# A branch hint, one block ahead, for the branch that skips each expert's overflow block

## The chip, the cores and the metric

The kernel runs on one core of one Trainium2 chip. The metric is the device time of one execution in microseconds (us); the kernel before took 1608.27 us in the median of three executions (1607.67 to 1610.89).

## What is computed

Two transformer blocks over 256 tokens of 1024 features, batch 1, in float32. The first block has two layers: gated linear attention and a mixture of experts, then a linear recurrence (LRU) and a second mixture of experts. The second block is a merge of three mixers and a convolutional feed-forward. What the change touches is the mixture of experts: a router picks experts for each token, and each of 16 experts computes, for its own tokens,

```python
# per expert e, for the tokens routed to it
y = (silu(x @ w_gate[e]) * (x @ w_up[e])) @ w_down[e]
out[token] += weight * y
```

How many tokens an expert gets is known only when the kernel runs.

## The kernel before, in words

The function `moe` (line 826) runs twice, once per layer. Each expert has 64 fixed slots for tokens: `gather` (L864) brings the tokens of four experts into slots by a product with a one-hot matrix, `gate_up` (L875) multiplies the slots with the gate and up weights, `transp` (L884) turns the result, `down` (L914) multiplies with the down weights, ScalarE (L922) and VectorE (L925) scale the result into two parts `y`, and `scatter` (L931) adds them onto the accumulator in PSUM. An expert with more than 64 tokens needs 32 slots more: the overflow block, that is `block_x` (L959 to L977), `block_up` (L984 to L991) and `block_down` (L998 to L1005). An expert with more than 96 tokens needs a loop over further blocks, `blocks` (L1014 to L1030).

Whether the overflow block runs is decided on the chip. `nblk` holds the number of extra blocks of each expert, every engine loads it into a register (L844), and a `tc.If(vals[e] > 0)` makes all five engines branch. For three experts of each layer, e = 0, 1 and 15 (`split`), the block is cut in two tests: gathering and the up product at L1049, the down product at L1068. For the other thirteen there is one test, at L1068. So an engine meets 19 tests per layer and 38 in all. Where the test is false the engine jumps over the code of the block to a short arm that only counts up its semaphore (the EVENT_SEMAPHORE rows of L1068 and L1049), and goes on behind it.

The code is straight-line: nothing but these tests and the loop inside `blocks` jumps. A scheduler orders the instructions of each engine between two tests; it moves none across a test. So, on TensorE (PE), after the test of one expert come typically the scatter of that expert, the transposes of the next expert's hidden values, most of the gate-up product of the one after, the down product, and the next test.

The weights (2 MB tiles, three per expert) are loaded by SyncE (SP) through one DMA queue in the order of use, into nine tiles during a mixture; `self.ws.free(3)` at an expert's end lets the loads of a later expert start.

Of the kernel before, what the change touches and what calls it, by code (L numbers as in the profile page):

```python
# [145 lines left out]
class Stream:  # L146
    """the weights in the order of their use, loaded ahead into as many tiles as there are"""
# [5 lines left out]
    def add(self, pool, n, until=None):  # L153
        """n tiles of the pool, for the weights before those named `until`"""
        if until:
            self.until[pool] = until
        self.open += [pool] * n
        self.fill()
# [38 lines left out]
class Banks:  # L197
    """the PSUM in two pools, for tiles of two names"""
# [8 lines left out]
class Act:  # L207
    """activations [features, tokens] as two float32r parts whose sum they are"""
# [6 lines left out]
class Half:  # L215
    """features in two tiles of 4"""
# [9 lines left out]
class Acts(Act):  # L226
    """an Act in four tiles"""
# [6 lines left out]
class Net:  # L234
# [39 lines left out]
    def weights(self, n, until=None):  # L274
        """n more tiles for the weights before the mark `until`"""
        self.wB.close()
        if n:
            p = self.wB.enter_context(self.tc.tile_pool(name="wB", bufs=n, side="right"))
            self.ws.add(p, n, self.marks.get(until))
# [112 lines left out]
    def lru_rates(self, pool):  # L392
        """-8 * softplus(-lambda) / 2, and half the gates' biases: sigmoid(z) is (1 + tanh(z / 2)) / 2"""
        nc = self.nc
        cl = self.cl = self.const.tile([P, 8], F32, name="cl")
        cm = pool.tile([P, 8], F32, name="cm")
        lam = self.p("lru_lambda")
        nc.scalar.activation(cl, lam, AF.Abs)
        nc.scalar.activation(cl, cl, AF.Exp, scale=-1.0)
        nc.scalar.activation(cl, cl, AF.Ln, bias=1.0)  # L400
        nc.vector.tensor_scalar(cm, lam, -1.0, 0.0, op0=OP.mult, op1=OP.max)
        nc.vector.tensor_tensor(cl, cl, cm, op=OP.add)
        nc.vector.tensor_scalar(cl, cl, -4.0, None, op0=OP.mult)
        for n in ("lru_b_r", "lru_b_i"):
            nc.vector.tensor_scalar(self.p(n), self.p(n), 0.5, None, op0=OP.mult)

# [1 line left out]
    def conditions(self, pool):  # L408
        """the conditions c, c_2 and c_ctx_2 after their silu, as columns of the array"""
        nc = self.nc  # L410
        s = self.cond = pool.tile([P, KT, 32], F32, name="cond")
        nc.vector.memset(s, 0.0)
        for i, n in enumerate(("c", "c_2", "c_ctx_2")):
            nc.scalar.activation(s[:, :, i], self.p(n), AF.Silu)

    def mod_tile(self, name, j, ps, sb):
        """512 of the modulation vectors, for each of the conditions; the columns of the array take a part of the sum each"""
# [21 lines left out]
    def rsqrt(self, out, x, sb, factor=None):  # L439
        """out = factor * x ** -0.5, x positive: a guess from the exponent and three steps of Newton"""  # L440
# [15 lines left out]
    def rstd(self, out, sums, n, sb, factor=None):  # L456
        """out = factor * (sums / n + eps) ** -0.5, for each token"""
# [4 lines left out]
    def sumsq_by_4(self, x, lhs, n, ps, sb):  # L462
        """[tokens, 2, n]: the squares of x, weighted with the first n columns of the 32 of lhs(k), summed over the
        features; the columns of the array take a part of the sum each"""
# [23 lines left out]
    def sumsq_steps(self, x, ps, sb):  # L488
        """the same into the PSUM, a feature tile at a time: the squares of all but the last tile are added up before"""
# [20 lines left out]
    def rows(self, col, ps):  # L510
        """[any partition, tokens] (PSUM) from [tokens, 2]"""
# [10 lines left out]
    def norm_mod(self, h, x, g, shift, scale, ps, sb, g0=None, between=None, st=None, rw=None):  # L522
        """h = modulated rmsnorm of x; in two parts if h is an Act; with g0, x is first replaced by its rmsnorm;
        between is called between the halves of the features; st: the sums of the squares, rw: the tokens' factors, if
        they are there"""
# [42 lines left out]
    def ctx_norm(self, hc, mc, ps, sb):  # L568
        """hc = modulated rmsnorm of the context, which comes with the weights"""
# [47 lines left out]
    def proj_T(self, out, pc, act, k0=0):  # L617
        """out [128 features, tokens] from a piece [features in, 128 features]"""
# [4 lines left out]
    def lin_T_by_k(self, w, act, ps):  # L623
        """lin_T with one act, all the products together as the features of the act come"""
# [11 lines left out]
    def lin_T(self, w, acts, ps, n=None, pool=0):  # L636
        """for each 128 columns of the weights: a product with each of acts; the low parts of the first `pool` pieces
        made by GpSimd"""
# [12 lines left out]
    def lin_tok(self, w, act, ps, outs=None, k0=0, k1=8):  # L651
        """[tokens, 512] for both tiles of tokens"""
# [24 lines left out]
    def open_route(self):  # L677
        """what a mixer shares with the routing after it"""
# [5 lines left out]
    def gla(self):  # L684
        nc, tc = self.nc, self.tc
        with ExitStack() as st:
# [23 lines left out]
            # the bias as a 17th row  # L710
# [115 lines left out]
    def moe(self, l, m, late, aside={}):  # L826
        nc, tc = self.nc, self.tc
        shift, gate = m[:, 24:32], m[:, 40:48]
        with ExitStack() as st:
# [59 lines left out]
            def slots_of(e, pt):  # L889
                """[slot, token]: 1 where the slot is the token's"""  # L890
# [7 lines left out]
            def slot_w(g):  # L898
                """the weights of the slots, for the experts of a group"""
# [8 lines left out]
            def down(heT, wd, wsl):  # L908
# [9 lines left out]
                # both parts of the results below each other, for one pass  # L918
# [25 lines left out]
            def tokens_of(oo, rk):  # L944
                """[token, slot]: 1 where the token is the slot's; rk: ranks less those of the slots before"""
# [4 lines left out]
            def block_x(e, oo):  # L950
                """32 more slots of an expert whose weights are there.
                A quarter of the features, at last of the results, on each 32 of the array's columns"""
# [61 lines left out]
            def blocks(e):  # L1014
                """the slots of an expert from the 97th on"""
# [16 lines left out]
            # all the products onto zeros, whether the banks count as written or not  # L1032
# [6 lines left out]
            for e in range(NE):  # L1039
# [5 lines left out]
                split, end = e in (0, 1, NE - 1), e == NE - 1  # L1045
                tokens_of(oo, rank64[:, e, :])
                he, last = gate_up(lambda k: XG[g][:, k, j, :], W[e])
                if split:
                    with tc.If(vals[e] > 0):  # L1049
                        blocks(e)  # L1050
                        block_x(e, oo)
                        block_up(e, "pgu")
                    self.ws.free(3 if more else 2)
                pt = ps.tile([P, 512], F32, name="ps")
                heT = transp(he, pt)
# [12 lines left out]
                with tc.If(vals[e] > 0):  # L1068
# [15 lines left out]
    def route_ahead(self, l, m):  # L1084
        """what the routing needs of a feature tile of x, to be called with each as soon as it is there"""
# [32 lines left out]
    def route(self, hh, hl, whl, rank, nblk, late):  # L1118
        """the normed tokens [tokens, features] in two parts, without the norm's gain and the modulation; which experts'
        slots they go to (rank), with which weights"""  # L1120
# [21 lines left out]
        def behind(v, n, name):  # L1142
            """how many of the four, of each of n fours, come before each: the larger ones and the earlier equal ones"""
# [28 lines left out]
        # the blocks of 32 slots after the first 64  # L1172
# [21 lines left out]
    def lru(self, m):  # L1194
        nc, tc = self.nc, self.tc
        with ExitStack() as st:
# [34 lines left out]
            # the gates as 2 * sigmoid - 1  # L1231
# [69 lines left out]
    def to_tok(self, dst, src, n, ps):  # L1301
        """dst [tokens, 2, n * 128] from src [features, n, tokens]"""
# [7 lines left out]
    def to_feat(self, dst, src, ps):  # L1310
        """dst [features, 4, tokens] from src [tokens, 2, 512]"""
# [69 lines left out]
    def merge(self, nm, mrg, h, y, ps, mx, first, slots, m=None):  # L1381
        """mrg += 2 * sigmoid(h @ w_gate) * (y @ w_branch); at last m, its half in two parts"""
# [33 lines left out]
    def y_act(self):  # L1416
        """4 tiles of features, in turn in the two halves of a tile"""
# [6 lines left out]
    def scalar_gates(self, nm, act, pc, ea, ps, mx):  # L1424
# [10 lines left out]
        # softplus: of the forget gates' negative, of the steps  # L1435
# [8 lines left out]
        # token rows: forward heads at columns 0..3, backward ones at 32..35  # L1444
# [13 lines left out]
        # cum: up to and with the token; aft: what follows it; tot: the tile's sum; per direction, in a tile of 128  # L1458
# [11 lines left out]
        # the rows of the forget and input gates, and the running maximum over the sequence  # L1470
# [34 lines left out]
    def conv_silu(self, dst, px, cw, ft, cb, mx):  # L1505
        """silu of the convolution; its weights and biases are halved"""
# [7 lines left out]
    def ctx_states(self, hc, gates, ps, mx, norm):  # L1514
        """what the context leaves: the states of both scans in both directions, keys and values"""
# [85 lines left out]
    def decays(self, pr, E, far, near, ncol, colx, prev):  # L1601
        """E[:, 0] over all t from the tile `far` of s, E[:, 1] over the tile `near` of t from the same of s, E[:, 2]
        from before the sequence; pr holds the part of t, in rows"""
# [14 lines left out]
    def masked(self, sm, pq, st, scale):  # L1618
        """scaled scores of the tile st of s: [:, direction, st, t]"""
# [116 lines left out]
    def tok_out(self, y, src, ps):  # L1736
        """y, in features, from src [tokens, 2, 512]"""
# [9 lines left out]
    def ssd(self, hT, L, C, y, ps, mx):  # L1747
# [72 lines left out]
        # gated with silu(z): here twice that, and half in the norm  # L1820
# [46 lines left out]
    def qk_tok(self, dst, pq, nm, rot, mx, scale=None):  # L1867
        """normed (and turned) queries or keys [tokens, 2, 512]; with scale the norm's factor times it, not applied"""
# [114 lines left out]
    # the features in between whose products with w_down follow those of w_up  # L1983
    DOWNS = {1: ((0, 4),), 3: ((4, 4),), 5: ((8, 4),), 7: ((12, 4),), 10: ((16, 4), (20, 2))}

    def ffn(self, h, m2):
        nc, tc = self.nc, self.tc
        with ExitStack() as st:
# [11 lines left out]
            for i in range(11):  # L2000
                w = self.ws.take("up")
                out = lambda: ps.tile([P, 512], F32, name="pd").rearrange("p (a t) -> p a t", a=2)
                if i == 0:
                    # as the features of h come
# [29 lines left out]
                for k0, nk in self.DOWNS.get(i, ()):  # L2034
                    w = self.ws.take("down")
                    # the last ones by features out, to be done with some of them earlier
# [104 lines left out]
```

## Time and profile before

| | |
|---|---|
| median of 3 executions | 1608.27 us (1607.67 to 1610.89) |
| profiled execution: span, first to last instruction | 1602.8 us |
| its own time, span and what lies around it | taken as the median, 1608.3 us: 5.5 us lie around the span |
| first mixture of experts | 219 to 523 us of the span |
| LRU mixer | 523 to 686 us |
| second mixture of experts | 686 to 971 us |
| second block | 971 to 1602 us |
| DMA of instructions, TensorE's queue | 134 packets, 2.20 MB |

How to read it: the profile has each engine's busy time, what ended each wait, and the clock that TensorE was granted as a share of its full rate. PEq, DVEq, ACTq and SPq are the sequencers of the engines, which fetch instructions, branch and count semaphores ahead of what the engine itself computes; PEld is TensorE's loading of weights into the array. A wait "<- issue" is one for which the profile shows no releaser: the instruction was not yet there. Matmuls of float32 appear as two records each.

### The profile page before, as it was taken

How to read it: one execution, taken by the hardware profiler on the slowest of the kernel's cores; microseconds unless marked ns; L12 is line 12 of the kernel's file. 1: busy time of each engine (PE TensorE's matmuls, PEld its weight loads, DVE VectorE, ACT ScalarE, POOL GpSimd, SP SyncE). 2: the span in 40 equal slices, each digit the busy share in tenths (PEclk: the TensorE clock that was granted, in tenths of full speed). 3: DMA queues.
4: the chain of work that ended last, by engine and by line, in shares of the span. 5: the costliest groups of instructions: out<-in, count | busy, mean ns of one | idle time of the engine just before them, and what ended most of it. 6: DMA issues, size and time to landing. Idle time of an engine off the chain costs nothing. (4 is left out here: it accounts for less than half of the span.)

```text
span 1602.8 us, 23900 instructions
## 1 busy us (share of the span) xinstructions
PE 1453.8 (91%) x9234; PEld 1001.7 (62%) x9234; DVE 806.0 (50%) x1926; ACT 659.6 (41%) x1347; POOL 85.6 (5%) x84
## 2 busy tenths in 40 slices
PE   6999979977878889889887988999999999999999
PEld 3565734333333568634332436888888889889998
DVE  3444432111211776522223125887876787777676
ACT  3634432111211575512121215666664565555553
POOL 0000110000000042200000000000000101400000
PEclk9999989999999999999998999999999999999999
DMA  9998687969999687786979846544643734896400
GB/s 364 387 371 311 222 332 253 350 233 349 354 341 382 218 294 284 279 326 229 392 287 358 319 160 239 187 145 171 205 163 106 262 106 142 301 348 201 142 1 27
DMA packets 193155, 406.44 MB, mean 254 GB/s; under 512 B 4513, under 2 KB 30753, under 8 KB 192690
## 3 DMA queue, kind: packets, MB, share of 16 engines
q1 hardware_dynamic: 192192, 402.75, 69.8%
q8 instruction: 134, 2.20, 0.6%
q10 hardware_dynamic: 754, 0.88, 0.2%
q14 instruction: 75, 0.61, 0.1%
HBM read 402.57 MB, written 1.05 MB: 252 GB/s over the span
## 5 line engine op out<-in xcount | busy, mean ns | idle before, releaser
L604 DVE TENSOR_TENSOR piece<-wt,piece 128x512 fp32r<-128x512 f32 (+1 forms) x364 | 278.0, 769 | 149.3 <-ACT piece L603 147.7
L603 ACT ACTIVATE piece<-wt 128x512 fp32r<-128x512 f32 (+1 forms) x368 | 248.5, 680 | 209.4 <-PE pd L615 158.6
L875 PE MATMUL pgu<-wt,xg 128*64 128x512 f32 x1024 | 266.0, 642 | 25.9 <-PEq L1068 19.8
L875 PEld LDWEIGHTS pgu<-wt,xg 128*64 128x64 f32 x1024 | 77.6, 146 | 162.3 <-issue 152.8
L614 PE MATMUL pd<-hT,piece 128*128 128x256 f32 x624 | 177.7, 285 | 0.0
L615 PE MATMUL pd<-hT,piece 128*128 128x256 f32 x624 | 177.6, 286 | 0.0
L613 PE MATMUL pd<-hT,piece 128*128 128x256 f32 x624 | 177.4, 285 | 0.0
L914 PE MATMUL py<-wt,heT 128*64 128x512 f32 x512 | 130.8, 624 | 5.0 <-ACT heT L886 3.3
L894 DVE TENSOR_SCALAR sa<-ps,par_cst 128x256 fp32r<-128x256 f32 x32 | 15.5, 484 | 231.9 <-issue 170.7
L615 PEld LDWEIGHTS pd<-hT,piece 128*128 128x128 f32 x624 | 118.4, 190 | 3.6 <-issue 1.8
L922 ACT ACTIVATE y<-py,wsl 64x512 fp32r<-64x512 f32 x64 | 43.8, 684 | 185.7 <-PE py L914 168.7
L614 PEld LDWEIGHTS pd<-hT,piece 128*128 128x128 f32 x624 | 118.7, 190 | 2.1 <-issue 2.0
L613 PEld LDWEIGHTS pd<-hT,piece 128*128 128x128 f32 x624 | 118.7, 190 | 1.5 <-issue 1.2
L425 PE MATMUL pd<-wt,cond 128*32 128x512 f32 x576 | 88.4, 630 | 0.9 <-DMA wt<-ada_w 0.9
L914 PEld LDWEIGHTS py<-wt,heT 128*64 128x64 f32 x512 | 39.4, 143 | 74.1 <-issue 68.0
L878 ACT ACTIVATE he<-pgu 128x256 f32<-128x256 f32 x32 | 12.3, 385 | 166.0 <-PE pgu L875 156.7
L931 PE MATMUL acc<-sa,y 128*128 128x256 f32 x256 | 43.5, 309 | 40.2 <-PEq L1068 21.8
L931 PEld LDWEIGHTS acc<-sa,y 128*128 128x128 f32 x256 | 35.2, 201 | 66.5 <-issue 44.9
L613 PE MATMUL pd<-s,piece 128*128 128x256 f32 x224 | 66.2, 297 | 2.3 <-ACT s L1242 2.3
L614 PE MATMUL pd<-piece,hT 128*128 128x512 f32 x160 | 65.8, 412 | 0.1
L615 PE MATMUL pd<-s,piece 128*128 128x256 f32 x224 | 65.0, 294 | 0.7 <-POOL piece L601 0.6
L614 PE MATMUL pd<-s,piece 128*128 128x256 f32 x224 | 64.7, 291 | 0.4 <-DVE s L609 0.4
(591 smaller groups left out, 2936.6 us busy)
## 6 DMA issues: line engine op xcount, KB each, us to landing
wt<-moe_w_gate SPq DMA_DIRECT2D x64, 1024.0 KB, 9.3
wt<-moe_w_up SPq DMA_DIRECT2D x64, 1024.0 KB, 11.6
wt<-moe_w_down SPq DMA_DIRECT2D x32, 2048.0 KB, 13.7
wt<-ada_w SPq DMA_DIRECT2D x24, 2048.0 KB, 16.7
wt<-w_in SPq DMA_DIRECT2D x21, 2048.0 KB, 9.2
wt<-w_mod SPq DMA_DIRECT2D x12, 2048.0 KB, 8.3
wt<-w_up SPq DMA_DIRECT2D x22, 1024.0 KB, 10.0
wt<-gla_w_in SPq DMA_DIRECT2D x6, 2048.0 KB, 19.7
```

The costliest lines, as they stand in the source:

```text
L425: nc.tensor.matmul(acc[32 * c:32 * c + 32, :], self.cond[:, k, :], w[:, k, :], start=(k2 == 0), stop=(k2 == 1))
L603: self.cast = nc.scalar.activation(hi, v, AF.Copy).ins
L604: (nc.gpsimd if low_on_pool else nc.vector).tensor_tensor(lo, v, hi.bitcast(F32), op=OP.subtract)
L613: mm(out, l[0], r[0], start=start, stop=False, **k)
L614: mm(out, l[0], r[1], start=False, stop=False, **k)
L615: mm(out, l[1], r[0], start=False, stop=stop, **k)
L875: last = nc.tensor.matmul(pgu[64 * hf:64 * hf + 64], xg(k), w[k // 4][:, :, k % 4, 256 * hf:256 * hf + 256], start=(k == 0), stop=(k == KT ...
L878: nc.scalar.activation(he, pgu[:, 0, :], AF.Silu)
L894: nc.vector.tensor_scalar(sa, pt[:, :T], self.c("slotcol"), None, op0=OP.is_equal)
L914: nc.tensor.matmul(py[64 * c:64 * c + 64, :], heT[:, b, 64 * hf:64 * hf + 64], wd[:, 2 * hf + b, 512 * c:512 * c + 512], start=(n == 0), s ...
L922: nc.scalar.activation(y[0:64, c], py[h], AF.Copy, scale=wsl[h])
L931: nc.tensor.matmul(acc[:, ft, :], y[:, ft // 4, ft % 4 * P:ft % 4 * P + P], sa, start=False, stop=False, skip_group_check=True)
```

## The change

Each test gets a label, and `mark_branch_hint_location` asks for an instruction BRANCH_PREFETCH_HINT on all five engines that names the test's branch and says that it will likely be taken, that is, that the engine will jump over the block. The instruction names no condition and waits for nothing. The rest of the diff takes comments out of the file.

```diff
@@ in moe, the loop over the experts
                 W[e] = [self.ws.take("moe") for _ in range(3)]
                 split, end = e in (0, 1, NE - 1), e == NE - 1
+                tc.mark_branch_hint_location(f"up{l}_{e}" if split else f"ex{l}_{e}", "LikelyTaken", engines=[mybir.EngineType.PE, mybir.EngineType.SP, mybir.EngineType.DVE, mybir.EngineType.Activation, mybir.EngineType.Pool])
                 tokens_of(oo, rank64[:, e, :])
                 he, last = gate_up(lambda k: XG[g][:, k, j, :], W[e])
                 if split:
-                    with tc.If(vals[e] > 0):
+                    with tc.If(vals[e] > 0, label=f"up{l}_{e}"):
                         blocks(e)
                         block_x(e, oo)
                         block_up(e, "pgu")
                     self.ws.free(3 if more else 2)
                 pt = ps.tile([P, 512], F32, name="ps")
+                if split:
+                    tc.mark_branch_hint_location(f"ex{l}_{e}", "LikelyTaken", engines=[mybir.EngineType.PE, mybir.EngineType.SP, mybir.EngineType.DVE, mybir.EngineType.Activation, mybir.EngineType.Pool])
                 heT = transp(he, pt)
...
-                with tc.If(vals[e] > 0):
+                with tc.If(vals[e] > 0, label=f"ex{l}_{e}"):
                     if not split:
                         block_x(e, oo)
                         block_up(e)
```

Where the hints land is shown by the order of TensorE's instructions. First an unsplit expert in the first layer, from the end of the overflow block before it (the first row is the jump that closes that block) to its own test. Before:

```order
L1068 UNCONDITIONAL_BRANCH
L931 MATMUL acc<-sa,y 128x256 x8
L884 MATMUL ps<-par_pk_70,he 128x128 x2
L875 MATMUL pgu<-wt,xg 64x512 x13
L914 MATMUL py<-wt,heT 64x512 x8
L892 MATMUL ps<-par_pk_70,rank 128x128 x2
L875 MATMUL pgu<-wt,xg 64x512 x3
L844 TENSOR_LOAD nblk
```

And now (the lines of the file are three further down):

```order
L1071 UNCONDITIONAL_BRANCH
L2138 BRANCH_PREFETCH_HINT
L931 MATMUL acc<-sa,y 128x256 x8
L884 MATMUL ps<-par_pk_70,he 128x128 x2
L875 MATMUL pgu<-wt,xg 64x512 x13
L914 MATMUL py<-wt,heT 64x512 x8
L892 MATMUL ps<-par_pk_70,rank 128x128 x2
L875 MATMUL pgu<-wt,xg 64x512 x3
L844 TENSOR_LOAD nblk
L1071 COMPARE_AND_BRANCH
```

The hint is the first instruction that the engine meets after the jump over the block before, and one expert's work lies between it and its branch. No matmul has moved.

Second the split expert 0 of the first layer, between its two tests, as it is now:

```order
L1050 UNCONDITIONAL_BRANCH x2
L2138 BRANCH_PREFETCH_HINT x2
L884 MATMUL ps<-par_pk_70,he 128x128 x2
L914 MATMUL py<-wt,heT 64x512 x8
L892 MATMUL ps<-par_pk_70,rank 128x128 x2
L1071 COMPARE_AND_BRANCH
L998 MATMUL pgu<-wt,oht 32x256 x16
```

Two hints stand together here: the first names the up-test of expert 1, which comes after the one below, and the second names the test L1071 a few rows on. The order of the hinted branches is thus the reverse of the order of the hints. VectorE, ScalarE, GpSimd and SyncE have a hint at the same places, and nothing else differs in their order.

## Rows read from the trace of the kernel before

**Rows 1.** Busy time by stage: first mixture, LRU, second mixture.
```profile
core 0: us, PE busy (x) PEld busy (x) DVE busy (x) ACT busy (x) POOL busy (x), PEclk, DMA share, GB/s
219.00:523.00 304.00, 253.19 (x1302) 106.34 (x1298) 61.27 (x140) 49.33 (x96) 0.00 (x0) 0.93 0.87 320
...
686.00:971.00 285.00, 241.69 (x1183) 100.39 (x1183) 66.64 (x160) 53.90 (x108) 5.08 (x7) 0.95 0.80 294
```

**Rows 2.** Waits of PE: line, releaser, us in total, times, longest us.
```profile
PE acc L931 <- PEq L1068: 21.8, 13, 3.2
PE pgu L875 <- PEq L1068: 19.8, 8, 3.4
...
PE acc L931 <- issue: 11.7, 3, 4.6
...
PE ps L581 <- PEq L1068: 3.4, 1, 3.4
...
PE acc L931 <- PEq L1049: 2.5, 1, 2.5
```

**Rows 3.** Branch records of lines 1068 and 1049: ns minimum, median, maximum.
```profile
L1068 PEldq COMPARE_BRANCH  x33: 78/4979/6330, 224.5 to 965.7; - x33
L1068 DVEq COMPARE_BRANCH  x33: 47/56/63, 230.3 to 969.8; - x33
...
L1049 PEldq COMPARE_BRANCH  x7: 82/1926/6361, 218.7 to 959.8; - x7
```

**Rows 4.** Two single branches of L1068, and the DMA between start and end of each.
```profile
L1068 PEldq COMPARE_BRANCH  x1: 3765/3765/3765, 264.6 to 264.6; - x1
...
DMA packets 1, 0.02 MB, mean 4 GB/s; under 512 B 0, under 2 KB 0, under 8 KB 0
...
L1068 PEldq COMPARE_BRANCH  x1: 6049/6049/6049, 298.6 to 298.6; - x1
...
q1 hardware_dynamic: 841, 2.41, 101.5%
```

**Rows 5.** Straight code, 1003 to 1590 us: TensorE's code packets, and instructions run.
```profile
q8 instruction: 34, 0.56, 0.4%
...
1003.00:1590.00 587.00, 580.67 (x4312) 524.88 (x4311) 450.67 (x1060) 343.97 (x736) 30.63 (x23) 0.99 0.50 169
```

**Rows 6.** Overflow blocks that ran: L990 runs once in each, L984 on pgu if split.
```profile
L984 PE MATMUL pgu<-wt,oxg 128*32 128x256 f32 x64 | 3.7, 381 | 1.0 <-DVE oxg L976 1.0
...
L990 PE MATMUL ps<-par_pk,oxt 128*128 128x128 f32 x3 | 1.0, 328 | 2.2 <-DVE oxt L988 2.2
```

**Rows 7.** Timeline behind the branch of 315.2 us, VectorE and PE: start, us, instruction.
```profile
319.07 1.53 DVE L925 SCALAR_TENSOR_TENSOR y<-py,wsl,y 64x512 fp32r<-64x512 f32 x2 [0.19 <-ACT y L922]
320.63 0.42 DVE L879 TENSOR_TENSOR he<-he,pgu 128x256 f32<-128x256 f32 x1
...
317.83 1.93 PE L875 MATMUL pgu<-wt,xg 128*64 128x512 f32 x6
321.50 0.95 PE L931 MATMUL acc<-sa,y 128*128 128x256 f32 x6 [1.73 <-PEq L1068]
325.81 0.80 PE L931 MATMUL acc<-sa,y 128*128 128x256 f32 x2 [3.37 <-issue]
```

**Rows 8.** The same behind the branch of 418.7 us, PE.
```profile
424.95 1.90 PE L875 MATMUL pgu<-wt,xg 128*64 128x512 f32 x6 [3.03 <-PEq L1068]
```

**Rows 9.** Two stretches at half clock behind such waits; columns as in rows 1.
```profile
306.50:309.90 3.40, 3.40 (x10) 0.96 (x8) 0.00 (x0) 0.18 (x1) 0.00 (x0) 0.50 1.05 381
...
323.60:330.30 6.70, 4.49 (x12) 1.83 (x14) 0.00 (x0) 0.38 (x1) 0.00 (x0) 0.50 1.04 392
```

**Rows 10.** Waits that could come next: weights (PEld), VectorE's branch (PEld), SP's own.
```profile
PEld acc L931 <- DVEq L1068: 15.5, 6, 2.7
...
PEld pgu L875 <- DMA wt<-moe_w_gate: 3.3, 1, 3.3
...
SPq L177 <- PEq L1068: 139.4, 12, 19.7
```

## The prediction

> **What bounds the kernel now.** I read the stages first, then the waits of TensorE (PE), then single branches. By stage, PE is busy for 253.19 of the 304 us of the first mixture of experts and for 241.69 of 285 us of the second [rows 1]: these two stretches hold 51 and 43 us in which PE does nothing, and the granted clock there is 0.93 and 0.95 of full. DMA is at a share of 0.87 and 0.80, so neither stretch is bound by the weights all the time.
>
> The waits name the idle time. PE waits for its own sequencer at the test L1068 before the scatter L931 (21.8 us, 13 times), before the gate-up product L875 (19.8 us, 8 times) and once before L581 (3.4 us), once at L1049 (2.5 us); three more times, 11.7 us in all, it waits in the middle of the scatter for "issue", an instruction that is not there yet [rows 2]. Together 59.2 us.
>
> Why the sequencer is late is in the branch records [rows 3]. On PE one of L1068 takes 4979 ns in the median and 6330 at most, on VectorE 56 ns. The shortest on PE take 78 and 82 ns. What fills the long ones is a load of code: in the branch of 264.6 us, 3765 ns long, one packet of 16 KB is all that any DMA queue moves, and the branch of 298.6 us takes 6049 ns while the weights' queue keeps the 16 engines at 101.5% [rows 4]. So a jump over the block costs a fetch from memory, and the fetch queues behind the weights. In straight code PE's 8623 matmuls and weight loads between 1003 and 1590 us needed 34 such packets [rows 5], 254 instructions each, with PE busy for 580.67 of 587 us: what comes next in the file is loaded ahead, and what lies behind a jump is not. The code that is jumped over is some 500 instructions on PE, two packets: 125 matmul records (8 + 2 + 2 + 64 + 1 + 32 + 16, a float32 matmul being two) with as many weight loads, once in the block and once in its loop.
>
> PE itself does not idle for the whole branch, since its sequencer runs ahead of it: of the 6.0 us behind 315.2 us PE saw 1.73 us [rows 7], behind 418.7 us 3.03 us [rows 8].
>
> **The change part by part.** It adds 38 hints per engine, and removes and moves nothing else. If a hint makes the code behind the jump come early, the branch should fall from about 5 us to near the 0.08 us of one that goes straight on [rows 3]; between hint and branch lies about one expert's work, 253.19 / 16 = 16 us [rows 1], against 6.4 us for the slowest branch [rows 3].
>
> *Gain, waits.* The upper end is all of the 59.2 us [rows 2]. Not all can go, since VectorE is late next: behind the branch of 315.2 us PE's idle time begins at 321.50 - 1.73 = 319.77 us, but VectorE finishes y at 319.07 + 1.53 = 320.60 and he at 320.63 + 0.42 = 321.05, and only then comes its own branch of 0.06 us [rows 3, 7]. The scatter needs that y and waits for VectorE's count, which the trace shows as DVEq L1068 six times [rows 10]. About 321.1 - 319.8 = 1.3 us stay in each of the six, 8 us. Where gate-up follows the branch, as at 418.7 us, nothing of the sort is due and the wait goes whole [rows 8]. The 3.37 us at "issue" [rows 7] go too: the sequencer has just landed near the end of a block and waits for the next one, and if it lands 6 us earlier that load is done in time. Taken: 59.2 - 8 = 51.
>
> [...]
>
> *Loss, wrong hints.* Three overflow blocks ran, one of them in a split expert [rows 6]: 4 of the 38 tests go straight on, where the hint says otherwise. Now they cost 0.08 us. If the hinted code has taken the place of the next block, PE waits as in the "issue" waits, 11.7 / 3 = 3.9 us [rows 2]; if not, nothing. Between 0 and 16 us; taken 2 us each, 8.
>
> *Loss, weights.* Up to now PE waits for a weight tile once, 3.3 us, and SP waits for PE to free tiles, 139.4 us in the first mixture [rows 10]. A faster PE frees tiles sooner and so asks more of the DMA: the first mixture keeps it busy for 0.87 x 304 = 264 us, and as much at the highest share seen, 1.05 [rows 1, 9], takes 252 us. With some 40 us less the stretch lasts 264 us, near that floor. Between 0 and 12 us lost; taken 5.
>
> *Loss, paired hints.* Behind the up-test of a split expert two hints stand together, and the one for the later branch comes first. If an engine keeps one hint alone, the later branch has none; the nearest such wait is the 2.5 us at L1049 [rows 2]. Taken 3 us, bounds 0 and 6.
>
> *The hints themselves* cost no more than a branch that goes straight on, 38 x 0.08 = 3 us on each sequencer. Taken as 0: PE's sequencer is ahead by the 3 us or so that separate a branch from the wait it causes, and the other engines wait for PE here. On VectorE, ScalarE, GpSimd and SP a branch takes 0.06 us or less [rows 3] or is off PE's path, so the hints there gain nothing.
>
> [...]
>
> *Sum:* 51 + 18 - 8 - 5 - 3 = 53 us less. The profiled execution has a span of 1602.8 us, and 5.5 us around it if its own time is the median of the three runs, 1608.27: 1608.3 - 53 = 1555. With the bounds of the terms the main case lies between 1529 (51 + 28) and 1591 (51 - 16 - 12 - 6).
>
> **Rivals.** *Half of the hints are lost.* From the hint to the branch PE issues, in an expert without a gather, 60 matmuls (8 + 2 + 32 + 16 + 2) with their weight loads, 120 instructions, and with a gather of eight feature tiles about 200, against 254 per block [rows 5]. So in 47% and 79% of the cases an edge between two blocks lies in between: for the 24 unsplit tests that jump, 18 x 0.47 + 6 x 0.79 = 13. If the load of the next block at the edge throws the hinted one out, only the other eleven gain: 11/24 of 69 us less 5 is 27 us, 1581 us. For it: the trace shows one block loaded ahead, never two. Against it: a hint that can be given an expert earlier would be of little use then.
>
> *Nothing happens.* The hint is not acted on, or names the arm that comes next anyway: 1608 us. For it: no hint ran in the trace of before, so nothing shows that one works. Against it: the branch that it names has a jump only in the arm that skips.
>
> *Slower: the hinted block takes the place of the next one.* On PE, wherever an edge lies between hint and branch, the engine then finds no code at the edge, loads it, drops the hinted block, and waits again at the branch. Each such edge costs the uncovered 3.9 us [rows 2] and its share of clock, 39% of some 3.4 us or 1.3 us [rows 9]: 13 x 5.2 = 68 us more, against 11/24 x 69 = 32 us gained, and 4 wrong hints do not matter beside it: 36 us slower, 1644 us. It decides from about nine such edges on (9 x 5.2 = 47 against 15 x 2.9 = 43). For it: only one block ahead is ever seen loaded, and code loads queue behind the weights [rows 4]. Against it: a hint given early and lost at each edge would defeat itself.
>
> **How the numbers follow.** Main case 0.53; half 0.14; nothing 0.14; slower 0.19. About 0.2%, 3.2 us, is what a measurement of this kernel can tell from no change. Faster is the first two, 0.67; within 0.2% is the third, 0.14; slower 0.19. The likeliest is 1555 us, with 1529 to 1591 of its own. The range reaches up over the half and the nothing cases to 1611 and leaves the slower one out, 0.19: 1530 to 1611.
>
> **What would show it.** Right: the median of PE's branch records falls from 4979 to a few hundred ns; "PEq" and "issue" nearly vanish from PE's waits before L875 and within L931; waits on VectorE's branch or on y of about 1.3 us take their place before L931; the clock rises above 0.97 in both mixtures; the first mixture lasts about 265 us with DMA near a share of 1; PE's code packets stay near the 134 of the table. Half: long branches stay where an edge lies ahead of them. Slower: new "issue" waits amid L875, L914 or L864 and more code packets. The forecast is wrong if branches shrink and the mixtures do not, because the weights or VectorE hold PE; or if they do not shrink.

## The result and the profile after

The changed kernel took 1553.32 us (median of 4 executions, 1551.34 to 1554.58), the kernel before 1608.62 (4 executions): a ratio of 0.9654, 95% interval 0.963 to 0.9677. The forecast was 1555. The profiled execution has a span of 1552.8 us, 50.0 less than before. It took 1554.58 us itself, so only 1.8 us lie around its span, not the 5.5 that the table of before has; if 1.8 holds there too, the execution profiled before took about 1604.6 us (an estimate), less than any of the four. So 55.3 us by the medians and 50.0 by the two profiles are the same change, seen beside a slower and a faster execution of before.

Busy time by stage, first and second mixture; the columns after the length are PE, PEld, DVE, ACT and POOL busy, the granted clock, the DMA share and GB/s:

```profile
219.00:497.50 278.50, 247.30 (x1306) 105.38 (x1306) 61.57 (x141) 49.24 (x96) 0.00 (x0) 0.94 0.92 344
...
663.00:921.00 258.00, 233.75 (x1186) 98.02 (x1185) 67.36 (x163) 53.83 (x108) 5.17 (x7) 0.97 0.87 325
```

Beside [rows 1] the first mixture is 304.0 - 278.5 = 25.5 us shorter and the second 285 - 258 = 27. In both together PE's idle time falls from 50.8 + 43.3 = 94.1 us to 31.2 + 24.3 = 55.5, by 38.6, and its busy time by 5.9 + 7.9 = 13.8: with the same matmuls that is the clock, up from 0.93 and 0.95 to 0.94 and 0.97. The LRU stretch between them is 165.5 us long, 2.5 more than before, and the second block is the same, which leaves the 50.0.

The branch records (ns minimum, median, maximum; the lines of the file moved by up to three):

```profile
L1071 PEldq COMPARE_BRANCH  x33: 74/439/6418, 225.3 to 914.5; - x33
...
L1071 DVEq COMPARE_BRANCH  x33: 47/61/80, 231.1 to 918.6; - x33
...
L1050 PEldq COMPARE_BRANCH  x7: 74/3506/6239, 219.5 to 908.9; - x7
```

The exit test's median on PE went from 4979 ns [rows 3] to 439; but some are still 6.4 us long, and the up-test's median rose. PE's waits (us in total, times, longest):

```profile
PE ps L959 <- issue: 6.7, 1, 6.7
PE pgu L875 <- PEq L1071: 6.4, 8, 3.7
PE acc L931 <- PEq L1050: 5.1, 2, 2.6
...
PE acc L931 <- PEq L1071: 4.4, 15, 0.4
...
PE ps L581 <- DVE oo L947: 3.6, 1, 3.6
...
PE acc L931 <- DVE y L925: 3.0, 2, 2.7
```

Of the 59.2 us of [rows 2], the 41.6 behind L1068 at L931 and L875 are now 10.8, and the 11.7 at issue are 0.4 at L931. Two did not go: the 2.5 at the up-test are 5.1, and the 3.4 at L581 are 3.6 (now put on VectorE's `oo`; a branch of 6.4 us still stands right ahead of it). The wait at L959, 1.3 us before, is 6.7. TensorE's code packets fell from 134 to 122:

```profile
q8 instruction: 122, 2.00, 0.5%
```

How PE now goes through the scatter (ACT's and DVE's y, then PEld and PE; start, us):

```profile
314.76 1.38 ACT L922 ACTIVATE y<-py,wsl 64x512 fp32r<-64x512 f32 x2 [9.27 <-PE py L914]
316.17 1.53 DVE L925 SCALAR_TENSOR_TENSOR y<-py,wsl,y 64x512 fp32r<-64x512 f32 x2 [0.18 <-ACT y L922]
317.14 1.21 PEld L931 LDWEIGHTS acc<-sa,y 128*128 128x128 f32 x8 [1.15 <-DVE y L925]
317.15 1.41 PE L931 MATMUL acc<-sa,y 128*128 128x256 f32 x8 [0.28 <-PEq L1071]
```

It is the expert of [rows 7]. Its 1.73 and 3.37 us are 0.28 and none. The scatter begins at 317.15, before the second half of y is finished at 316.17 + 1.53 = 317.70 and before VectorE's branch: it waits for neither. What TensorE's weight loading waits for, 1.15 us, is the first half of y; PE itself idles for 0.28, which the profile puts on its sequencer.

### The profile page after: what moved, and what is told of

It is laid out like the page before. It is cut to its first block, busy times and chain, and to the rows that moved or that the text cites. A ratio compares the mean times of both kernels' runs of the same rounds, so it can differ in the third digit from the quotient of the medians.

```text
span 1552.8 us, 24090 instructions
## 1 busy us (share of the span) xinstructions
PE 1439.3 (93%) x9234; PEld 997.2 (64%) x9234; DVE 806.0 (52%) x1926; ACT 659.3 (42%) x1347; POOL 85.8 (6%) x84
## 5 line engine op out<-in xcount | busy, mean ns | idle before, releaser
L604 DVE TENSOR_TENSOR piece<-wt,piece 128x512 fp32r<-128x512 f32 (+1 forms) x364 | 277.3, 768 | 151.7 <-ACT piece L603 150.2
L875 PE MATMUL pgu<-wt,xg 128*64 128x512 f32 x1024 | 250.1, 611 | 11.6 <-PEq L1071 6.4
L875 PEld LDWEIGHTS pgu<-wt,xg 128*64 128x64 f32 x1024 | 73.8, 139 | 136.3 <-issue 130.3
L914 PE MATMUL py<-wt,heT 128*64 128x512 f32 x512 | 130.4, 625 | 3.3 <-ACT heT L886 3.3
L894 DVE TENSOR_SCALAR sa<-ps,par_cst 128x256 fp32r<-128x256 f32 x32 | 15.5, 484 | 200.4 <-issue 138.0
L914 PEld LDWEIGHTS py<-wt,heT 128*64 128x64 f32 x512 | 39.3, 142 | 71.5 <-issue 65.3
L614 PE MATMUL pd<-piece,hT 128*128 128x512 f32 x160 | 65.7, 412 | 0.1
L615 PE MATMUL pd<-piece,hT 128*128 128x512 f32 x160 | 63.3, 398 | 0.0
L613 PE MATMUL pd<-piece,hT 128*128 128x512 f32 x160 | 58.7, 412 | 3.8 <-ACT piece L603 3.7
## 6 DMA issues: line engine op xcount, KB each, us to landing
wt<-moe_w_up SPq DMA_DIRECT2D x64, 1024.0 KB, 13.3
wt<-moe_w_down SPq DMA_DIRECT2D x32, 2048.0 KB, 15.5
```

The lines of the kernel that those rows point to most:

```text
L604: (nc.gpsimd if low_on_pool else nc.vector).tensor_tensor(lo, v, hi.bitcast(F32), op=OP.subtract)
L613: mm(out, l[0], r[0], start=start, stop=False, **k)
L614: mm(out, l[0], r[1], start=False, stop=False, **k)
L615: mm(out, l[1], r[0], start=False, stop=stop, **k)
L875: last = nc.tensor.matmul(pgu[64 * hf:64 * hf + 64], xg(k), w[k // 4][:, :, k % 4, 256 * hf:256 * hf + 256], start=(k == 0), stop=(k == KT ...
L914: nc.tensor.matmul(py[64 * c:64 * c + 64, :], heT[:, b, 64 * hf:64 * hf + 64], wd[:, 2 * hf + b, 512 * c:512 * c + 512], start=(n == 0), s ...
```

## The experiments

Each ratio is to the kernel before in the same series of runs; the change itself stands at 0.9654.

| run | median us | ratio, 95% interval |
|---|---|---|
| e1_pe_only | 1550.25 | 0.9655 (0.9633 to 0.9677) |
| e2_rest_only | 1597.59 | 0.9954 (0.9934 to 0.9973) |
| e3_one_hint | 1544.78 | 0.9627 (0.9601 to 0.9653) |
| e4_no_wrong | 1550.08 | 0.9654 (0.9631 to 0.9677) |
| f1_one_pe | 1545.51 | 0.9605 (0.9577 to 0.9633) |
| f2_early | 1561.12 | 0.9709 (0.9682 to 0.9735) |
| f3_late | 1549.96 | 0.9647 (0.9615 to 0.9678) |
| f4_shift | 1534.65 | 0.9547 (0.9515 to 0.9579) |
| g1_before_shift | 1598.74 | 0.9942 (0.992 to 0.9964) |
| g2_sp_only | 1599.58 | 0.9951 (0.9932 to 0.997) |
| g3_shift24 | 1536.67 | 0.9578 (0.9548 to 0.9607) |
| h1_early_aligned | 1530.3 | 0.9516 (0.9488 to 0.9543) |

### Which engine's hints: e1 and e2

```diff
-... engines=[mybir.EngineType.PE, mybir.EngineType.SP, mybir.EngineType.DVE, mybir.EngineType.Activation, mybir.EngineType.Pool])
+... engines=[mybir.EngineType.PE])
```

> Hints on TensorE alone. Theory (the gain is TensorE's code behind the jump coming ahead; the other engines' branches of 0.06 us have nothing to gain): the same time as the change, 1553 us, within 3 us. Rival (the other engines' hints carry a part, or cost some time on the DMA that the weights need): 1560 to 1600 us in the first case, 1545 to 1549 in the second.

The ratio is that of the change, 0.9655 beside 0.9654: TensorE's hints are enough for all of it. e2 has the other four in the same place.

> Hints on VectorE, ScalarE, GpSimd and SyncE, none on TensorE. Theory: the time before, 1608 us, within 4 us, and TensorE's branches of the exit test back at a median near 5 us. Rival (the four engines' hints matter): below 1600 us.

0.9954: PE's branches are long again, as the theory has it, but the time is 0.5% below that of before, and its interval leaves 1 out. The theory's 1604 to 1612 is missed; the rival's "below 1600" is met by the number, 1597.59, but the kernel before took 1605.17 in this series, and 0.9954 of 1608 is 1600.6. Neither side had a gain of this size. The branch record of e2, and its waits:

```profile
L1071 PEldq COMPARE_BRANCH  x33: 70/5637/6338, 225.5 to 960.3; - x33
```

```profile
PE acc L931 <- PEq L1071: 25.6, 13, 3.1
PE pgu L875 <- PEq L1071: 15.6, 6, 3.6
...
PE ps L884 <- issue: 4.2, 1, 4.2
...
PE ps L959 <- issue: 2.1, 1, 2.1
```

The waits on the sequencer are those of before. What went are the 11.7 us at issue amid L931 [rows 2]; in their place stand 4.2 and 2.1 elsewhere. In the compiled program TensorE's code of e2 differs from that of before in one mark at each of the 38 places that the hinted tests jump to, and in nothing else. That suggested that the code lies elsewhere in memory, which g1 and g2 took up.

### The place of the code: g1 and g2

g1 is the kernel before with dead code: transposes in the loop over further blocks, which no expert of this input enters.

```diff
                             nc.tensor.transpose(pt[:, tt * P:tt * P + P], rank[:, tt, e:e + 1].to_broadcast([P, P]),
                                                 self.ident)
+                        if (l, e) == (0, 2):
+                            for _ in range(48):
+                                nc.tensor.transpose(pt[:, T:T + P], rank[:, 0, e:e + 1].to_broadcast([P, P]), self.ident)
```

> The kernel before, without any hint, with the 48 transposes in the loop that does not run: all code behind the first layer's expert 2 lies 96 instructions later. Theory (the three waits for issue of before, 11.7 us, fall on landings a few instructions ahead of the end of a block of code, and so depend on where the code lies): these three are gone from the experts 5 and 8 of the first layer and 6 of the second, at most one or two stand elsewhere, and the time falls by 3 to 9 us, to 1599 to 1605 beside 1608. Rival (the waits belong to those experts, whatever the place of the code): they stay, and 1608 within 3 us.

> Hints on SyncE alone, which only issues loads and waits for TensorE. Theory (the 7 us that the hints on four engines gained without TensorE's come from TensorE's own code lying elsewhere, since the program of TensorE differs from that of before in nothing but the marks of its 38 jump targets): the same gain, 5 to 9 us, ratio 0.995. Rival (they come from the hints of VectorE, ScalarE or GpSimd): the time before, ratio 0.998 to 1.002.

Both as the theory said, g1 at the edge of its range (1598.74 beside 1599 to 1605): 0.9942 without any hint, 0.9951 with hints on an engine that has nothing to gain by them. The three waits are gone from their experts; of g1's waits

```profile
PE ps L884 <- issue: 3.8, 1, 3.8
```

is the largest at issue. So 0.5 to 0.6% of the time, 7 to 10 us in e2, g1 and g2, hangs on where the code lies. The change's gain of 3.46% probably holds such a part too: against e2, whose marks are the same, TensorE's hints give 0.9655 / 0.9954 = 0.970, 3.0% or 48 us. This is not the hints alone, since the 38 hint instructions also move TensorE's code, by up to 38 instructions; but without hints on TensorE no other place of its code has moved the time by more than 10 us.

### One hint at a time: e3

```diff
                     self.ws.free(3 if more else 2)
                 pt = ps.tile([P, 512], F32, name="ps")
-                if split:
-                    tc.mark_branch_hint_location(f"ex{l}_{e}", "LikelyTaken", ...)
                 heT = transp(he, pt)
```

> The hint for the second test of the split experts 0, 1 and 15 is left out, so that the hints for the next expert's test stand alone and not first of a pair. Theory (an engine keeps one hint, the later one): the four branches at 235, 266, 678 and 709 us of the profile, 3.4 to 6.2 us long with the pairs, fall to about 0.4 us, and the up-test of the second layer's expert 0 (3.5 us) too; the waits of TensorE behind them, 2.5 + 0.3 + 2.6 + 0.4 + 1.4 = 7.2 us, go, and the time falls by 4 to 8 us to about 1547. Rival (a hint is dropped at the taken jump that lies between, since the second test of the split expert jumps before the hinted branch comes): these branches stay at 3 to 6 us, and the time stays at 1553 or rises a little, since the second tests lose their hints.

The five branches fell to 0.32 to 0.35 us. The up-tests, and the exit test of expert 2, whose record at 265.5 us was 3351 ns long in the change:

```profile
L1050 PEldq COMPARE_BRANCH  x7: 78/339/3407, 219.5 to 901.4; - x7
```

```profile
L1069 PEldq COMPARE_BRANCH  x1: 318/318/318, 262.4 to 262.4; - x1
```

The jump of the split expert's second test still lies between hint and branch, so here the jump did not drop the hint (0.32 to 0.35 us in e3), and a second hint did (3.35 to 6.24 us for the same five in the change). The trace of e3 has it in order: hint for the first layer's up-test of expert 1 at 222.4 us, the jump at 225.3, a code packet on TensorE's queue at 228.7, the hinted branch at 235.1. The time is 5.5 us below e1 of the same series; the two intervals overlap, but f1, the same hints on TensorE alone, repeats it with 0.9605. The second tests lost nothing without theirs: their branches stay at 0.23 to 0.36 us. Their jump is 100 instructions, against 254 in a code packet [rows 5], so by my estimate its target lies in the block at hand or the next.

> One hint at a time and on TensorE alone, the two edits before together. Theory (the hints of the other engines neither gain nor cost beside TensorE's): the 1544.8 us of the run with one hint at a time, within 3 us. Rival (each hint instruction on the other engines costs something that the pairs hid): 1538 to 1541.

The theory holds, at 1545.51 us.

### Wrong hints: e4

```diff
+                go = (l, e) not in ((0, 6), (0, 15), (1, 12))
+                if go:
                     tc.mark_branch_hint_location(f"up{l}_{e}" if split else f"ex{l}_{e}", "LikelyTaken", ...)
...
-                if split:
+                if split and go:
                     tc.mark_branch_hint_location(f"ex{l}_{e}", "LikelyTaken", ...)
```

> No hints at the four tests that go straight on for this data (first layer: expert 6, and both tests of expert 15; second layer: expert 12). Theory (a wrong hint takes the place of the next block, so that the block that does run comes late): the wait of 6.7 us at the gathering of expert 15's overflow block goes or shrinks to that of a block edge, and the time falls by 5 to 10 us to 1543 to 1548. Rival (the wait there is a code load that has nothing to do with the hint): 1553 within 3 us, and the wait stays.

The rival holds. The time is that of e1 (1550.08 beside 1550.25, each uncertain by some 3.7), and the wait stays:

```profile
PE ps L959 <- issue: 5.2, 1, 5.2
...
PE ps L959 <- DVEq L1016: 1.3, 1, 1.3
```

It belongs to another jump: inside the block the test L1016 jumps over the loop, has no hint, and lands wherever the code lies (in the change its branch on TensorE takes 3.80 us at 466.1 us, and 0.34 in the other two blocks). The wait at L959 is 1.3 us on VectorE's branch alone in before and in f4, where the code lies elsewhere, 3.5 on L1016 in f2 and g3, and 6.7 in the change.

### When a hint comes too late, and where: f3, f4 and g3

f3 gives the hint of an unsplit expert behind the down product (`self.dl` is its last matmul) and no longer at the head of the loop:

```diff
...
+                if not split:
+                    with tc.issue_after(self.dl):
+                        tc.mark_branch_hint_location(f"ex{l}_{e}", "LikelyTaken", engines=[mybir.EngineType.PE])
                 with tc.If(vals[e] > 0, label=f"ex{l}_{e}"):
```

> As the one-hint run on TensorE, but the hint of an unsplit expert stands behind its down product, 18 to 39 instructions and some 2 to 4 us ahead of its branch (137 or 109 for the three experts of a layer that are followed by gathering). Theory (the hinted code needs 5 to 8 us from the hint under the weights' load, and a hint that comes later than that gains nothing): 18 of the 24 jumps of unsplit experts take 4 to 6.4 us again, the six with the long distance 0.35 to 0.5; the time is 1580 to 1600 us. Rival (a hint works as soon as it is given, or a branch joins the load that the hint began and is shorter by the lead): branches of 2 to 4 us, which are within what TensorE's queue covers, and 1545 to 1560 us.

My 1580 to 1600 was wrong; 1549.96 is within the rival's range, though eight branches of 6 us remain where the rival had 2 to 4. The records of a hint 2.1 us ahead of its branch, and of one 3.0 us ahead:

```profile
L2141 PEldq BRANCH_PREFETCH_HINT  x1: 36/36/36, 372.6 to 372.6; - x1
...
L1074 PEldq COMPARE_BRANCH  x1: 6039/6039/6039, 374.7 to 374.7; - x1
...
L2141 PEldq BRANCH_PREFETCH_HINT  x1: 36/36/36, 430.3 to 430.3; - x1
...
L1074 PEldq COMPARE_BRANCH  x1: 3380/3380/3380, 433.4 to 433.4; - x1
```

The first gained nothing: TensorE's code packet comes at 378.2 us, 3.5 behind the start of the branch, as without a hint (3.6 at the branch of 298.6 us in before). The second branch ends 6.4 us after its hint, about as long as a branch with a whole load beside the weights (6.05 us in [rows 4], 6.42 in the change), and its packet comes at 434.2, 3.9 behind the hint: it seems to have waited for a load that the hint had begun. Why 2.1 us of lead gain nothing and 3.0 gain nearly all of it is not shown. And a branch of 2 to 3.4 us cost PE next to nothing, since its sequencer is that far ahead: PE waits 0.3 us at L875 for the second one, 3.38 us long, and in f4, where the longest exit branch takes 3.72 us, no wait on the sequencer at L1072 is longer than 0.4. Six of the eight branches of 6 us stand ahead of the scatter; beside the nine short ones at 0.3 they cost (11.7 - 2.7) / 6 = 1.5 us each:

```profile
PE acc L932 <- PEq L1074: 11.7, 15, 1.8
```

f4 is f1 with the 48 transposes of g1, and g3 with 24.

> As the one-hint run on TensorE, with 48 transposes more in the loop over further blocks of the first layer's expert 2, which does not run here: the code of everything behind it lies 96 instructions later. Theory (the branches that stay long do so because their hint comes too late, 6.4 to 6.7 us ahead for the experts 10 and 9 with 94 instructions between): the same branches stay long, 6.2 to 6.4 us for expert 10 of the first layer and 9 of the second, and the time is within 3 us of that run. Rival (it is where the edges of the 256-instruction blocks lie): these two fall to 0.4 us, and others become long; the time moves by up to 8 us either way.

> As the one-hint run on TensorE with its code moved, by 24 transposes (48 instructions) in place of 48 (96). Theory (with all hints in place, what is left to gain lies in where the code is: the wait of 6.4 us in expert 15's overflow block, and the two branches of 6.2 us of the experts 10 and 9): the time lies between the two runs, 1534 to 1546, with each of these three waits either there or gone; each that is gone takes 3 to 6 us off. Rival (the 11 us of the run moved by 96 come from something else, such as the clock): 1545 within 3 us with the waits gone, or 1535 with the waits there.

The rival of f4 holds in kind: the two branches of experts 10 and 9 fell, to 2.5 and 2.0 us and not to 0.4, and others grew (2.75 us for expert 3 of the first layer, 0.35 in f1); the wait at issue before L959 is gone, and the time is 10.9 us below f1 where the rival had up to 8 (0.9547 beside 0.9605, intervals that barely touch). g3 is within its range at 1536.67; it has both branches at 2.7 and 2.4 us, the wait at L959 at 3.5, and a new one of 6.26 us, expert 7 of the second layer, whose hint came 15.5 us ahead. Time is no excuse there.

### Edges between blocks of code: f2 and h1

f2 gives each hint one test earlier, and at the head of the loop only that of expert 0:

```diff
...
+                if not end:
+                    with tc.issue_after(last):
+                        n = e + 1
+                        tc.mark_branch_hint_location(f"up{l}_{n}" if n in (1, NE - 1) else f"ex{l}_{n}", "LikelyTaken", engines=[mybir.EngineType.PE])
                 with tc.If(vals[e] > 0, label=f"ex{l}_{e}"):
```

> As the run before, but each hint one test earlier: the hint for expert e + 1 stands behind the jump of expert e - 1, ahead of the test of expert e, so that it has two experts' work of time, 25 us. Theory (an engine keeps one hint, and a new one takes the place of the old one whether or not its code is loaded already): the hint for e is overwritten in the same stretch of code in which the code of e should be fetched or was fetched, most exit branches go back to 3 to 6 us, and the time to 1580 to 1608 us. Rival (code that was fetched stays until the jump, and only the hint not yet served is overwritten): all exit branches at 0.35 to 0.45 us, also those of expert 10 in the first layer and 9 in the second that now take 6.3 us, and up-tests of expert 15 too; 1532 to 1540 us.

Neither: 1561.12, 12 of the 24 jumps of unsplit experts at 3.4 to 6.4 us and 12 at 0.34 to 0.48:

```profile
L1074 PEldq COMPARE_BRANCH  x33: 73/438/6408, 225.1 to 922.3; - x33
...
PE acc L931 <- PEq L1074: 15.9, 15, 3.2
PE pgu L875 <- PEq L1074: 11.0, 8, 3.5
```

For a rule I counted TensorE's instructions in the compiled program, cut them into blocks of 256 from one unknown start (an estimate: a code packet of 16 KB comes to 254 matmuls and weight loads in [rows 5], 255 with the 54 semaphore rows that TensorE's sequencer has there), and let a marked jump target that lies up to 16 instructions short of an edge start on it; with 0, 8, 24 or 32 in place of 16, one to four branches do not fit. Then ten neighbouring starts sort all 20 branches that stand behind neither a split expert nor a block that ran: the 9 long ones have an edge between the landing of the jump before and the branch, the 11 short ones have none. (The expectation of h1 has 7 and 11.) The same count, from one of these starts, orders the change's own 24 jumps of unsplit experts:

| last edge before the branch | since the landing before | jumps | length, us |
|---|---|---|---|
| 4 and 5 instructions | 8.9, 9.4 us | 2 | 6.37, 6.42 |
| 20 and 26 | 13.3, 11.5 | 2 | 1.69, 2.00 |
| 67 to 187 | | 6 | 0.35 to 0.53 |
| none since the landing | 9.2 to 10.7 | 3 | 2.83 to 2.89 |
| none since the landing | 11.8 and more | 9 | 0.34 to 1.22 |
| the hint lost in a pair | | 2 | 3.35, 3.87 |

The 6.26 us of g3 has its edge 11 instructions ahead. So the target seems to be loaded only when the engine is in the block that holds the branch. TensorE's code packets bear this out: between the landing at 750.9 us and that branch at 770.7 there is one, at 754.3, before the hint of 755.2 is given, and the next comes at 774.4, inside the branch. The DMA view from 750.9 to 770.6 us:

```profile
q8 instruction: 1, 0.02, 0.4%
```

In f2, by this rule, an edge in between means more than a late load: by the time the engine enters the block of the branch, the hint for the test behind it has taken the place of this one. The 12 long branches of f2 fit that, but no run shows it by itself. And a hint given behind the landing was served behind the load of the next block: for the first layer's experts 12 and 14 of the change, with no edge, landing to branch and branch add up to 10.7 + 2.8 = 13.5 and 10.5 + 2.9 = 13.4 us, two loads in a row (for expert 12 the packets are at 426.9 and 434.5 us). This rule came after the fact; h1 tests it ahead, with its own number (`PAD`) of dead transposes for each expert.

```diff
...
+                        for _ in range(PAD.get((l, e), 0)):
+                            nc.tensor.transpose(pt[:, T:T + P], rank[:, 0, e:e + 1].to_broadcast([P, P]), self.ident)
```

> The early hints of the run f2_early (1561 us, half of its jumps long) with dead transposes in the loops that do not run, 5 to 115 for each expert of both layers, so many that by count the jump of every unsplit expert lands at the start of a 256-instruction block and no edge of a block lies between a landing and the next test. Theory (formed from f2_early: on entering a block the engine loads the block that follows and then the target of the kept hint, if the hinted branch lies in the entered block; of 18 jumps there, the 7 long ones have an edge between landing and branch and the 11 short ones none, if the block count starts at any of ten places): all 24 jumps of unsplit experts take 0.3 to 0.6 us, those of expert 10 in the first layer and 9 in the second too, TensorE's waits on its sequencer before L875 and L931 fall to 0.4 us each, and the time is 1524 to 1534 us. Rival (the early hint is overwritten or not by chance or by time): about half the jumps stay at 3 to 6 us and the time at 1550 to 1565 us.

All 24 are between 0.33 and 0.50 us, the two of experts 10 and 9 among them:

```profile
L1079 PEldq COMPARE_BRANCH  x1: 402/402/402, 395.0 to 395.0; - x1
...
L1079 PEldq COMPARE_BRANCH  x1: 412/412/412, 789.9 to 789.9; - x1
```

```profile
PE acc L934 <- PEq L1079: 4.3, 15, 0.3
...
PE pgu L878 <- PEq L1079: 2.3, 8, 0.3
```

```profile
220.46:479.29 258.83, 238.81 (x1294) 101.63 (x1290) 60.82 (x141) 49.31 (x96) 0.00 (x0) 0.99 0.92 346
644.16:891.58 247.42, 228.27 (x1170) 96.44 (x1169) 65.56 (x158) 52.54 (x106) 5.17 (x7) 0.98 0.89 331
```

1530.3 us, a ratio of 0.9516 beside 0.9709 of f2, which has the same hints, and 0.9654 of the change, with the three intervals apart: the lowest ratio of the study, though f4's interval overlaps with it. One up-test stayed long, that of the second layer's expert 0, 3.47 us. It was in no fit, and by the same count an edge lies 5 instructions ahead of it; the branch took 2.60 us in f4 (25 instructions) and 0.35 in f1 and g3 (some 200 and more).

One part of h1's theory fails all the same. Where the hint is there at the landing, the target comes first and the next block second: before the branch of 395.0 us, 0.40 us long, one packet has come since the landing at 385.7, so it held the target, and the second begins with the branch. The DMA view from 385.7 to 395.0 us:

```profile
q8 instruction: 1, 0.02, 0.7%
```

## Why the prediction was right, and where it was not

*Sum.* 53 us forecast, 55.3 measured by the medians and 50.0 by the profiles. The terms by the windows of both mixtures: waits less the three losses, 51 - 8 - 5 - 3 = 35, measured 38.6; clock 18, measured 13.8. That this comes so close is partly luck, since wrong terms offset each other. Three losses of 8, 8 and 5 us that I subtracted (VectorE's y, wrong hints, weights) left little or no trace, and against them stand waits that I had counted as gone: 6.4 + 4.4 + 5.1 us on TensorE's sequencer and 3.6 at L581, and 6.7 - 1.3 = 5.4 us more at L959. Of the signs that I named, the branch's median came. The waits on the sequencer fell but did not vanish; the clock stopped at 0.94 in the first mixture, which lasted 278.5 and not 265 us; the second gave more than I had left for it; and the code packets fell from 134 to 122, where I had them stay near 134. No run shows the 18 us of clock in the forecast's sum, or the 28 of its upper bound, as a term of its own: what the windows show in its place is PE's busy time lower by 5.9 and 7.9 us, at a clock up by 0.01 and 0.02.

*The mechanism* held: the code behind the jump comes ahead, PE's branch falls to 0.4 us, and what TensorE waited for was this (e1 against e2). The hints on the other engines gain nothing, as said.

*"The 3.37 us at issue go too, if the sequencer lands 6 us earlier."* They went, but need no hint to go: they hang on the place of the code, and e2, g1 and g2 lose them with PE's branches as long as before. So some 8 us of the forecast gain was credited to the hints alone, where the marks that move the code are enough; which of the two took these waits away in the change itself is not shown.

*"About 1.3 us stay in each of the six scatters, 8 us."* Wrong: 0.28 us in the scatter shown, and at most 0.4 in each of the fifteen that wait behind L1071. I took VectorE's count from a wait that was inferred; the scatter starts on the first half of y and needs neither VectorE's product he nor its branch.

*Wrong hints, 8 us:* nothing that e4 can tell, 1550.08 without them beside 1550.25 in e1.

*Paired hints, 3 us:* right in kind, undersized: five branches lost their hint, and e3 gained 5.5 us beside e1.

*Weights, 5 us:* no sign of them. The DMA share rose to 0.92 and 0.87, and h1 brings the first mixture, from the first to the last branch, down to 258.8 us at 0.92, so the change was not bound by the weights at the 277.3 us that it takes between the same branches. My 264 us "near the floor" of 252 is thus undercut with no sign of a floor; whether there is one at 252 is not shown.

*The rivals.* "Half lost at an edge" had the edge matter the wrong way: g3's packets show no hinted block that an edge throws out, but a hint that is served only past the edge, and by the count only two branches of the change are hurt by it, 6.4 us each. "The hinted block takes the place of the next one" fell: the 0.4 us at issue amid L931 and none amid L875 or L914 show no missing next block. (Its 39% of clock is an estimate: half of the 3.40 + 4.49 us that PE was busy at a clock of 0.50, over 3.40 + 6.70 us [rows 9].) What the runs show of the jump itself: the median of the exit branch is 5.6 us with no hint on TensorE (e2) and 0.44 with one (the change).

What stays open: how a fetch is chosen when the next block and a target are both due (the rule is fitted, and tested ahead at one placement, where the order of the two loads came out otherwise), and why expert 13 of the second layer in f4, with its edge 3 instructions ahead, took 3.7 us and not 6.

## What to carry to other kernels

Where code is jumped over and the branch record is microseconds long on the engine that bounds the kernel, hint the branch on that engine alone, one hint at a time, with a load's time ahead (some 6.4 us beside busy weights here; where the hint stood behind a landing, 13.4 to 13.5 us from there). Then look at where the landing and the branch lie: the same hints gave a ratio of 0.9709 with edges between blocks in the way and 0.9516 without. Price a branch by the wait that it causes, not by its record: here one of 3.4 us cost PE 0.3 (f3). And a control with the hint on an engine that cannot gain tells how much of a gain is only moved code.

## What the runs showed that was not expected

Dead code that never runs moved the time by 0.6% (g1) and, with hints, by 0.7% (f4 against f1). TensorE kept one hint here, the last given, and it outlived a jump (e3: 0.32 to 0.35 us in place of 3.35 to 6.24). A hint seems to be served only in the block that holds its branch (g3: none of its load in 15.5 us ahead of the edge), and with no edge in the way all 24 jumps took 0.33 to 0.50 us (h1). A hint costs TensorE's sequencer 31 to 45 ns in the change.
